# Gate and branch products of a hybrid layer with tokens in the partitions, and one attention head beside each 512 gate columns

## The chip, the cores and the metric

The kernel runs on one core of one Trainium2 chip, and the metric is the device time of one execution in microseconds (us). The engines of a core are named as in the profile: PE (TensorE, matrix products; PEld is its loading of weights), DVE (VectorE), ACT (ScalarE), POOL (GpSimd) and SP (SyncE, which here only issues DMA transfers). Each engine runs its instructions in the order in which they stand in its queue; semaphores hold an instruction until what it reads is there and what it overwrites is no longer needed. Products accumulate in PSUM, which has eight banks of 512 float32 per partition; the kernel uses four as a rotating pool `acc`, and twice two as `aux0` and `aux1`.

## The reference

One layer of a hybrid backbone, for 256 latent tokens `x` and 256 context tokens, model width 2048. Everything is float32. What matters here is the merge of the two branches:

```python
h_l = modulate(rms_norm(x, norm1_w), sh1, sc1)
...                                   # gated linear attention -> ya (256 x 1024)
...                                   # differential attention, 8 heads of 128 -> yb (256 x 1024)
def merge(h, ya, yb):
    g_a, g_b = jnp.split(jax.nn.sigmoid(h @ w_gate + b_gate), 2, axis=-1)
    return (g_a * (ya @ w_proj_gla) + g_b * (yb @ w_proj_diff)) @ w_out
mix_l = merge(h_l, gla_out(...), diff_out(o_diff))
x_new = x + g1 * mix_l
x_new = x_new + g2 * conv_ffn(modulate(rms_norm(x_new, norm2_w), sh2, sc2), ...)
```

The gate product is 256 x 2048 by 2048 x 4096, the two projections together 256 x 2048 by 2048 x 2048 (the upper half of the contraction belongs to `ya`, the lower to `yb`), and `w_out` is 2048 x 2048. The modulation vectors `g1`, `sh2`, `sc2`, `g2` come from a product of the conditioning vector with `w_ada`, which DVE computes as dot products beside all other work.

## The kernel before

**Products in two halves.** Each float32 weight tile is split into a high half (`whi`, a cast on ACT, L206) and a low half (`wlo`, a subtraction on DVE, L213, in `split`), 512 columns at a time; activations are split in the same way. A product is high by high, high by low and low by high. Weights come through `fetch` (L225) in transfers of 512 KB, four buffers deep; the halves have four buffers each.

**Two forms.** `col_tile` (L238) makes 128 output columns, with these columns in the partitions: the weight half is the stationary operand, and one product of 512 columns (L262, `whi` with both halves of the 256 tokens side by side) and one of 256 (L264, `wlo`) make a contraction step of 128. The two halves of the bank are added later. `row_tile` (L276) makes 512 output columns for 128 tokens, with the tokens in the partitions: the activation is stationary and the weights stream, in three products of 512 columns. The values of both attentions (`dv_chunk`, L961, with `value_rows`) and the last stage (`down`) use this second form; queries, keys, gates, projections, `w_out` and the up stage use the first.

**The stages around the change.** `dv_chunk(0)`, four query tiles (`dq_tile`), `dv_chunk(1)`; then for each of the eight heads the attention (`scores`, L1001; `attend`, L1025) at a high priority for the scheduler, a further query tile after each of the first four, and three gate tiles (`gate_tile`, L1049); then the eight gate tiles that are left. The scheduler orders the instructions of each engine by program order, priority and its own estimate of times, so the order on the engines is not that of the source. Each `gate_tile` puts its sum plus the bias into half of a tile `C`, by ACT and DVE. Four tiles `ks` of the attention share their places with `C12` to `C15`, and all `C` tiles take the places of the context activations (`c0` to `c15`), which `dv_chunk(1)` reads last. Then `ya` is made from the linear attention's output and its gate (`ge`, L1091 to L1097), and for each of 16 blocks of 128 columns `col_tile` makes both projections (`pga`, `pgb`); sigmoid, two multiplications (one on POOL) and a sum follow, and `merged` (L1101) splits the sum into `A[c]`, the input of `w_out` (`mix`).

**Conditioning.** `ada_next(n)` (L672) adds n to a due count; for each whole one it issues a load of 512 KB of `w_ada` (`araw`, two buffers) on SP, and a dot product on DVE (L356) for the oldest load. Of the 128 such steps the gates take 21, by the table `GATE_ADA`.

Of the kernel before, what the change touches and what calls it, by code (L numbers as in the profile page):

```python
# [9 lines left out]
F32 = mybir.dt.float32  # L10
# [8 lines left out]
P = 128  # L19
# [29 lines left out]
for _n, _w in [("b_ada", 96), ("norm1", 16), ("norm2", 16), ("ba", 8), ("gonorm", 1), ("qnorm", 1),  # L49
               ("knorm", 1), ("donorm", 1), ("b_gate", 32), ("lam", 256), ("conv_w", 3 * 2 * FT),  # L50
               ("conv_b", 2 * FT)]:
    _VEC[_n] = (_o, _w)
    _o += _w
# [10 lines left out]
def _tiles(w, starts):  # L64

    k = w.shape[0]
    return np.ascontiguousarray(
        np.stack([w[:, s:s + P].reshape(k // P, P, P).transpose(1, 0, 2) for s in starts]))


# [4 lines left out]
def _lay_out(i):  # L75
# [19 lines left out]
    a["w_in"] = _tiles(w_in, starts)  # L95
    a["w_gate"] = _tiles(np.asarray(i["w_gate"])[0], range(0, 2 * D, P))
    pg, pd = np.asarray(i["w_proj_gla"])[0], np.asarray(i["w_proj_diff"])[0]
    a["w_proj"] = _tiles(np.concatenate([pg, pd], axis=0), range(0, D, P))
    a["w_out"] = _tiles(np.asarray(i["w_out"])[0], range(0, D, P))
# [19 lines left out]
        "donorm": np.asarray(i["diff_onorm_w"])[0][:, None],  # L119
        "b_gate": _vec_tiles(np.asarray(i["b_gate"])[0]),  # L120
        "conv_w": np.asarray(i["conv_w"])[0].reshape(3, 2 * FT, P).transpose(2, 0, 1).reshape(P, -1),
# [25 lines left out]
def layer_kernel(tc, I, out):  # L147
# [3 lines left out]
    with es:  # L151
# [129 lines left out]
        def value_rows(banks, ws, n, first, last, emptied):  # L281
# [12 lines left out]
            for t in range(4):  # L294
                for k, w in ws:
                    products(t, k, w)
                emptied(t)

# [396 lines left out]
        with tc.tile_pool(name="gla", bufs=1) as pg:  # L695
# [253 lines left out]
        with tc.tile_pool(name="diff", bufs=1) as pd:  # L949
# [11 lines left out]
            def dv_chunk(j):  # L961
# [7 lines left out]
                for q in turn:  # L969
# [78 lines left out]

            def gate_tile(j):  # L1049
                ada_next(GATE_ADA[len(gates)])  # L1050
                b = acc_bank("gate")
                col_tile(I["w_gate"][j], A, b)
                if j == len(C):
                    C.append(hp.tile([P, 2, T], F32, tag=f"c{j}", name=f"C{j}"))
                gates[j] = C[j % KT][:, j // KT, :]
# [7 lines left out]
            dv_chunk(1)  # L1063
            order = [j for k in range(KT) for j in (k, KT + k)]
# [35 lines left out]

        def merged(c, earlier):  # L1101
            i = V.tensor_tensor(gates[c], gates[c], gates[16 + c], op=ALU.add)
            after(i, earlier)
            split_act(A[c][:, 1, :], A[c][:, 0, :], gates[c])

        for c in range(KT):
            ba, bb = acc_bank("pga"), acc_bank("pgb")
            col_tile(I["w_proj"][c, :, 0:8, :], yap, ba)
            col_tile(I["w_proj"][c, :, 8:16, :], ybp, bb)
            for j in (c, 16 + c):  # L1110
                sigs.append(S.activation(gates[j], gates[j], AF.Sigmoid))
                after(sigs[-1], sigm)
                after(sigs[-1], copied[0])
            for b, j in ((ba, c), (bb, 16 + c)):
                t = p3.tile([P, T], F32, tag="pt", bufs=2, name="pt")
                i = added(t, b)
                (G if j > c else V).tensor_tensor(gates[j], t, gates[j], op=ALU.mult)
                if j == c and c:
                    merged(c - 1, i)
            if c < KT - 2:  # L1120
                ada_next(13 / (KT - 2))
        merged(KT - 1, i)
        ada_done(0)

# [239 lines left out]
```

## Time and profile before

| what | value |
|---|---|
| median of 3 runs | 1691.38 us (1690.87 to 1692.67) |
| the profiled execution | 1692.95 us, span of its instructions 1690.6 us |
| `dv_chunk(1)` and start of head 0 | up to 537.7 us (last `dvb`) |
| gate products | 542.6 to 775.5 us |
| projections | 775.8 to 865.0 us |
| `w_out` (`mix`) | 865.3 to 956.1 us |

The rows of the profile name a line, an engine, an operation and output<-inputs by the program's names. A row of groups ends in busy time and mean duration, then the idle time before the group and its cause. Products are pipelined: the end of each is modelled, and neighbours overlap, so the pace of a stream is read from starts and counts, and not from durations.

### The profile page before, as it was taken

The page shows a single profiled execution, that of the slowest core. Times are in us where ns is not written, and L with a number is a line of the kernel's source. Part 1 is how long each engine was busy: PE and PEld are TensorE (multiplying, and loading weights), DVE is VectorE, ACT ScalarE, POOL GpSimd, SP SyncE. Part 2 cuts the span into 40 slices and gives each one's busy share as a digit, 9 for nine tenths or more (in the row PEclk, how much of TensorE's full clock was granted, in tenths as well). Part 3 has the DMA queues.
Part 4 walks back from the last instruction along what each step waited for, and adds up shares of the span by engine and source line. Part 5 has one row for each costly group of instructions (what it writes and reads, how often), then busy time and mean ns, then how long its engine had stood idle before and what let it go on. Part 6 is the DMA issues. An engine that isn't in the chain of part 4 may idle for free.

```text
span 1690.6 us, 28643 instructions
## 1 busy us (share of the span) xinstructions
PE 1671.0 (99%) x10140; PEld 1442.3 (85%) x10140; DVE 1271.2 (75%) x2426; ACT 977.7 (58%) x1980; POOL 329.0 (19%) x431
## 2 busy tenths in 40 slices
PE   7999999999999999999999999999999999999998
PEld 6779999998777888888888998888888888888887
DVE  5556765867787978788998797878888787755655
ACT  5324554756345867656766686666666666544443
POOL 0000213131210000001323200222222222684000
PEclk9999999999999999999999999999999999999999
DMA  9995532435566555688877566667777776676664
GB/s 384 403 408 195 171 133 85 150 100 166 173 212 223 171 192 187 211 273 277 272 261 260 181 198 218 227 227 237 238 236 237 225 240 219 202 222 207 217 195 142
DMA packets 110831, 370.82 MB, mean 219 GB/s; under 512 B 14433, under 2 KB 19553, under 8 KB 110689
## 3 DMA queue, kind: packets, MB, share of 16 engines
q1 hardware_dynamic: 102112, 362.51, 64.2%
q10 hardware_dynamic: 4032, 4.37, 0.8%
q0 software_dynamic: 4544, 2.14, 0.6%
q8 instruction: 79, 1.29, 0.3%
q14 instruction: 64, 0.52, 0.1%
HBM read 364.73 MB, written 2.10 MB: 217 GB/s over the span
## 4 chain that ended last, share of the span: by engine, by line
PE 92%; DVE 3%; DMA 3%; issue 1%; ACT 1%; POOL 0%; SPq 0%; DVEq 0%; POOLq 0%; ACTq 0%
PE down L1317 14%; PE upg L262 9%; PE upv L262 9%; PE gate L262 7%; PE sweep L368 5%; PE upv L264 5%; PE upg L264 5%; PE gate L264 4%; PE mix L262 4%; PE ab L368 2%; PE mix L264 2%; PE pgb L262 2%; PE pga L262 2%; DMA araw<-in_w_ada 2%; PE dk L333 2%; PE dk L332 2%
## 5 line engine op out<-in xcount | busy, mean ns | idle before, releaser
L206 ACT CAST whi<-wraw 128x512 fp32r<-128x512 f32 (+2 forms) x1004 | 607.1, 608 | 386.6 <-DVE wlo L213 111.3
L213 DVE TENSOR_TENSOR wlo<-wraw,whi 128x512 fp32r<-128x512 f32 (+2 forms) x932 | 635.5, 690 | 224.3 <-ACT whi L206 217.0
L262 PE MATMUL upg<-a,whi 128*128 128x512 f32 x656 | 229.0, 391 | 0.0
L262 PE MATMUL upv<-a,whi 128*128 128x512 f32 x656 | 229.0, 391 | 0.0
L1317 PE MATMUL down<-whi,g 128*128 128x512 f32 x704 | 216.9, 389 | 0.0
L264 PE MATMUL upv<-a,wlo 128*128 128x256 f32 x656 | 182.8, 280 | 0.0
L264 PE MATMUL upg<-a,wlo 128*128 128x256 f32 x656 | 182.6, 280 | 0.0
L262 PE MATMUL gate<-a,whi 128*128 128x512 f32 x512 | 179.9, 397 | 0.0
L213 POOL TENSOR_TENSOR wlo<-wraw,whi 128x512 fp32r<-128x512 f32 x72 | 100.3, 1393 | 388.0 <-ACT whi L206 375.2
L356 DVE CUSTOM_DVE_ANT_0 araw<-araw,cb 128x1024 f32<-128x1024 f32 x128 | 160.4, 1254 | 12.5 <-DMA araw<-in_w_ada 12.5
L1317 PEld LDWEIGHTS down<-whi,g 128*128 128x128 f32 x704 | 132.1, 188 | 27.5
L262 PEld LDWEIGHTS upv<-a,whi 128*128 128x128 f32 x656 | 122.4, 187 | 26.6
L262 PEld LDWEIGHTS upg<-a,whi 128*128 128x128 f32 x656 | 122.4, 187 | 26.5
L264 PE MATMUL gate<-a,wlo 128*128 128x256 f32 x512 | 141.0, 285 | 0.0
L1317 PE MATMUL down<-wlo,g 128*128 128x512 f32 x352 | 136.9, 389 | 0.0
L264 PEld LDWEIGHTS upv<-a,wlo 128*128 128x128 f32 x656 | 123.9, 189 | 0.5
L264 PEld LDWEIGHTS upg<-a,wlo 128*128 128x128 f32 x656 | 123.9, 189 | 0.5
L262 PEld LDWEIGHTS gate<-a,whi 128*128 128x128 f32 x512 | 94.4, 188 | 19.8 <-issue 0.4
L264 PEld LDWEIGHTS gate<-a,wlo 128*128 128x128 f32 x512 | 96.6, 189 | 6.6 <-issue 1.9
L262 PE MATMUL mix<-a,whi 128*128 128x512 f32 x256 | 89.1, 397 | 0.0
L1317 PEld LDWEIGHTS down<-wlo,g 128*128 128x128 f32 x352 | 66.1, 188 | 13.6
L1290 POOL DMA_DIRECT2D row<-turned x128 | 69.3, 549 | 30.0 <-DVE turned L1286 18.1
(351 smaller groups left out, 3396.6 us busy)
## 6 DMA issues: line engine op xcount, KB each, us to landing
wraw<-in_w_up SPq DMA_DIRECT2D x164, 512.0 KB, 4.4
araw<-in_w_ada SPq DMA_DIRECT2D x128, 512.0 KB, 4.9
wraw<-in_w_down SPq DMA_DIRECT2D x88, 512.0 KB, 4.3
ada<-in_w_ad SPq DMA_DIRECT2D x64, 512.0 KB, 10.0
wraw<-in_w_gate SPq DMA_DIRECT2D x64, 512.0 KB, 4.5
wraw<-in_w_in SPq DMA_DIRECT2D x58, 512.0 KB, 4.0
wraw<-in_w_proj SPq DMA_DIRECT2D x32, 512.0 KB, 4.8
wraw<-in_w_out SPq DMA_DIRECT2D x32, 512.0 KB, 4.6
```

Of the source, the lines that this page charges most:

```text
L206: copied[0] = S.copy(hi[:, :n], raw)
L213: i = e.tensor_tensor(lo[:, :n], raw, hi[:, :n].bitcast(F32), op=ALU.subtract)
L262: i = PE.matmul(b.rearrange("p (a b) -> p a b", a=2), whi[:, sl], acts[k], start=first, stop=last)
L264: i = PE.matmul(b[:, T:], wlo[:, sl], acts[k][:, 1, :], start=False, stop=last)
L332: PE.matmul(o, whi[:, sl], lo[k], start=False, stop=False)
L333: i = PE.matmul(o, wlo[:, sl], hi[k], start=False, stop=last and j == 1)
L356: i = V.tensor_tensor_reduce(raw, raw, cb[:, q * 1024:(q + 1) * 1024], 1.0, 0.0, op0=ALU.mult, op1=ALU.add, accum_out=ada2[:, j, q:q + 1])
L368: return kept(PE.matmul(*args, **kw))
L1290: nc.gpsimd.dma_start(to[32 * (q % 4):32 * (q % 4 + 1), :, 32 * p:32 * (p + 1)], turned[32 * p:32 * (p + 1), :, 32 * q:32 * (q + 1)])
L1317: i = PE.matmul(banks[h][t][n], g[:, a, ts], w[n][b], start=k == 0 and (a, b) == (1, 0), stop=k == FT - 1 and b == 1)
```

## The change

Gates and projections go from the first form to the second. `gate_rows` makes eight chunks of 512 gate columns (in the order of the blocks: gate a, gate b of the first 512 channels, then of the next) for two times 128 tokens; `token_rows` takes one transfer of two contraction steps, splits it and makes 2 x 2 x 3 products of 512 columns. The bias is now along the free dimension, so it is loaded, repeated over the partitions, into the `C` tile (16 loads of 256 KB on SP), and one DVE addition of 512 columns per bank takes the place of ACT's and DVE's two of 256. One head stands beside each chunk, and the priority of the heads falls from 500 to 150. In the projections, four blocks of 512 columns for each branch are multiplied with the sigmoids on DVE alone; the merged sum then has the tokens in the partitions, and `turned` brings it back with 32 transposes on PE (`mT`, 128 x 128) from which `A` is split. The conditioning steps are spread anew: 0.75 in place of 0.5 per transfer of the GLA values, 12 in place of 8 in `dv_chunk(0)`, 12 in place of 16 in `dv_chunk(1)`, 21 evenly in the gates, 9 in place of 13 in the projections.

```diff
-GATE_ADA = [0.25] * 4 + [0.5] * 16 + [1] * 12
+GATE_ADA = [21.01 / 64] * 64
...
+        def token_rows(src, banks, acts, k0, first, last, emptied):
+            raw = fetch(src.rearrange("p a b -> p (a b)"), 1024)
+            def products(t, k, w):
+                hi, lo = [{k: acts[k][:, u, :]} for u in (1, 0)]
+                row_tile(banks[t], k, *w, slice(0, 512), hi, lo, slice(t * P, (t + 1) * P), k == first, k == last)
+            if k0 + 1 != last:
+                for a in range(2):
+                    w = split(raw[:, a * 512:(a + 1) * 512], 512)
+                    for t in range(2):
+                        products(t, k0 + a, w)
+                return
...
-                    ada_next(0.5)
+                    ada_next(0.75)
...
-                            if j or q > 3:
-                                ada_next(1)
+                            if j or q > 1:
+                                ada_next(0.75 if j else 1)
...
-            def gate_tile(j):
-                ada_next(GATE_ADA[len(gates)])
-                b = acc_bank("gate")
-                col_tile(I["w_gate"][j], A, b)
...
-                S.activation(gates[j], b[:, :T], AF.Identity, bias=vcol("b_gate", j))
-                V.tensor_tensor(gates[j], b[:, T:], gates[j], op=ALU.add)
+            def gate_rows():
+                for n in range(8):
+                    g = n // 2 + 4 * (n % 2)
+                    banks = [acc_bank("gate") for _ in range(2)]
+                    def emptied(t):
+                        V.tensor_tensor(gates[g, t], banks[t], gates[g, t], op=ALU.add)
+                    for q in range(8):
...
+                        if q == 5:
+                            for t in range(2):
+                                C.append(hp.tile([P, 2, T], F32, tag=f"c{len(C)}", name=f"C{len(C)}"))
+                                gates[g, t] = C[-1].rearrange("p a b -> p (a b)")
+                                nc.sync.dma_start(gates[g, t], I["b_gate"][:, g * 512:(g + 1) * 512])
+                        token_rows(I["w_gate"][g, q], banks, A, 2 * q, 0, KT - 1, emptied)
+                        yield
...
-                with tc.high_priority(500):
+                with tc.high_priority(150):
...
-                for _ in range(3):
-                    gate_tile(order.pop(0))
-            while order:
-                gate_tile(order.pop(0))
+                for _ in range(8):
+                    next(gating)
...
+        def turned(c):
+            for u in range(2):
+                b = aux_bank("mT", u)
+                for j in range(2):
+                    for t in range(2):
+                        PE.transpose(b[:, j * T + t * P:j * T + (t + 1) * P],
+                                     gates[c, t][:, (2 * u + j) * P:(2 * u + j + 1) * P], ident)
+                for j in range(2):
+                    a = A[4 * c + 2 * u + j]
+                    split_act(a[:, 1, :], a[:, 0, :], b[:, j * T:(j + 1) * T])
+        for c in range(4):
+            for part, acts in enumerate((yap, ybp)):
...
+                def emptied(t):
+                    V.tensor_tensor(gates[g, t], banks[t], gates[g, t], op=ALU.mult)
+                    if part:
+                        V.tensor_tensor(gates[c, t], gates[c, t], gates[g, t], op=ALU.add)
+                for q in range(4):
+                    if 8 * c + 4 * part + q < 28:
+                        ada_next(9.01 / 28)
+                    token_rows(I["w_proj"][c, 4 * part + q], banks, acts, 2 * q, 0, HEADS - 1, emptied)
+                if c and not part:
+                    turned(c - 1)
+        turned(3)
```

Three places of the engines' order show what the scheduler makes of it. First PE, in the gate stage beside a late head, before the change (`oss` is the sum for a head's norm, `s` its scores):

```order
L262 MATMUL gate<-a_1380,whi 128x512
L264 MATMUL gate<-a_1380,wlo 128x256
L614 MATMUL oss<-osqs,ones 128x256
L615 MATMUL oss<-osqs,ones 128x256
L1009 MATMUL s<-ks,qs 128x512 x6
L264 MATMUL gate<-a_1450,wlo 128x256
```

And PE beside one of the last three heads after the change:

```order
L1036 MATMUL s<-ks,qs 128x512 x2
L283 MATMUL gate<-whi,a_402 128x512
L1036 MATMUL s<-ks,qs 128x512
L284 MATMUL gate<-whi,a_402 128x512
L1036 MATMUL s<-ks,qs 128x512
L283 MATMUL gate<-whi,a_402 128x512
L1036 MATMUL s<-ks,qs 128x512
L284 MATMUL gate<-whi,a_402 128x512
L1036 MATMUL s<-ks,qs 128x512
L285 MATMUL gate<-wlo,a_402 128x512 x2
```

The six score products of a block, which stood together, now stand one by one between gate products; the gate products are all 512 wide, with the activation as the stationary operand.

Second PE, at the start of `w_out` after the change, where the last quarter of the merged sum is turned (`C_8175` and `C_8177` are its two halves of tokens); ahead of these rows stand 24 products of the first `mix` tile, on the quarters that are turned already:

```order
L268 MATMUL mix<-a_1133,whi 128x512
L270 MATMUL mix<-a_1133,wlo 128x256
L268 MATMUL mix<-a_219,whi 128x512
L1145 MATMUL mT<-ident,C_8175 128x128 x2
L1145 MATMUL mT<-ident,C_8177 128x128
L1145 MATMUL mT<-ident,C_8175 128x128
L1145 MATMUL mT<-ident,C_8177 128x128 x2
L1145 MATMUL mT<-ident,C_8175 128x128
L1145 MATMUL mT<-ident,C_8177 128x128
L270 MATMUL mix<-a_219,wlo 128x256
L268 MATMUL mix<-a_330,whi 128x512
```

The transposes moved behind the first products of `w_out`, with a second `mix` tile (from `a_219` on) taken in after them.

Third SP, late in `dv_chunk(1)` and at the first gate weights, after the change (`C_...` are the bias loads into the places of context tiles):

```order
L1095 DMA C_6981<-in_b_gate 128x512
L377 DMA araw<-in_w_ada 128x1024
L1095 DMA C_7335<-in_b_gate 128x512
L233 DMA wraw<-in_w_gate 128x1024
L1095 DMA C_7337<-in_b_gate 128x512
L377 DMA araw<-in_w_ada 128x1024
L1095 DMA C_7613<-in_b_gate 128x512
L233 DMA wraw<-in_w_gate 128x1024
L377 DMA araw<-in_w_ada 128x1024
L1095 DMA C_7615<-in_b_gate 128x512
L1095 DMA C_7894<-in_b_gate 128x512
L1095 DMA C_7896<-in_b_gate 128x512
```

Twelve of the sixteen bias loads stand here, ahead of the use of their tiles by up to six chunks; before the change SP had only weights and conditioning loads at this place.

More of the change, by code (lines that the diff above doesn't have):

```diff
@@ L49 @@
 for _n, _w in [("b_ada", 96), ("norm1", 16), ("norm2", 16), ("ba", 8), ("gonorm", 1), ("qnorm", 1),
-               ("knorm", 1), ("donorm", 1), ("b_gate", 32), ("lam", 256), ("conv_w", 3 * 2 * FT),
+               ("knorm", 1), ("donorm", 1), ("lam", 256), ("conv_w", 3 * 2 * FT),
                ("conv_b", 2 * FT)]:
@@ L68, in _tiles, with _row_tiles @@
         np.stack([w[:, s:s + P].reshape(k // P, P, P).transpose(1, 0, 2) for s in starts]))
+def _row_tiles(w):
+    k, n = w.shape
+    return np.ascontiguousarray(w.reshape(k // (2 * P), 2, P, n // 512, 512).transpose(3, 0, 2, 1, 4))
 def _vec_tiles(v):
@@ L95, in _lay_out @@
     a["w_in"] = _tiles(w_in, starts)
-    a["w_gate"] = _tiles(np.asarray(i["w_gate"])[0], range(0, 2 * D, P))
+    a["w_gate"] = _row_tiles(np.asarray(i["w_gate"])[0])
+    a["b_gate"] = np.tile(np.asarray(i["b_gate"])[0][None], (P, 1))
     pg, pd = np.asarray(i["w_proj_gla"])[0], np.asarray(i["w_proj_diff"])[0]
-    a["w_proj"] = _tiles(np.concatenate([pg, pd], axis=0), range(0, D, P))
+    a["w_proj"] = _row_tiles(np.concatenate([pg, pd], axis=0))
     a["w_out"] = _tiles(np.asarray(i["w_out"])[0], range(0, D, P))
@@ L119, in _lay_out @@
         "donorm": np.asarray(i["diff_onorm_w"])[0][:, None],
-        "b_gate": _vec_tiles(np.asarray(i["b_gate"])[0]),
         "conv_w": np.asarray(i["conv_w"])[0].reshape(3, 2 * FT, P).transpose(2, 0, 1).reshape(P, -1),
@@ L296, in value_rows @@
                     products(t, k, w)
+                emptied(t)
+        def token_rows(src, banks, acts, k0, first, last, emptied):
[9 more added lines that the diff above has]
+                return
+            ws = [split(raw[:, a * 512:(a + 1) * 512], 512) for a in range(2)]
+            for t in range(2):
+                for a in range(2):
+                    products(t, k0 + a, ws[a])
                 emptied(t)
@@ L1047, in layer_kernel @@
             gates, ya, yb = {}, {}, {}
-            def gate_tile(j):
-                ada_next(GATE_ADA[len(gates)])
-                b = acc_bank("gate")
-                col_tile(I["w_gate"][j], A, b)
-                if j == len(C):
-                    C.append(hp.tile([P, 2, T], F32, tag=f"c{j}", name=f"C{j}"))
-                gates[j] = C[j % KT][:, j // KT, :]
-                S.activation(gates[j], b[:, :T], AF.Identity, bias=vcol("b_gate", j))
-                V.tensor_tensor(gates[j], b[:, T:], gates[j], op=ALU.add)
+            def gate_rows():
+                steps = 0
+                for n in range(8):
[4 more added lines that the diff above has]
+                    for q in range(8):
+                        if q in (1, 2):
+                            flush((later, latest)[q - 1])
+                        ada_next(GATE_ADA[steps])
+                        steps += 1
+                        if q == 5:
[5 more added lines that the diff above has]
+                        yield
             nts = norm_tiles()
@@ L1063, in layer_kernel @@
             dv_chunk(1)
-            order = [j for k in range(KT) for j in (k, KT + k)]
+            gating = gate_rows()
             with tc.high_priority(500):
@@ L1099, in layer_kernel @@
         yap, ybp = [[y[h].rearrange("p (a b) -> p a b", a=2) for h in range(HEADS)] for y in (ya, yb)]
[L1101 to L1121, printed above, removed]
@@ L1122, in layer_kernel @@
-        merged(KT - 1, i)
+        def turned(c):
+            for u in range(2):
+                b = aux_bank("mT", u)
+                for j in range(2):
+                    for t in range(2):
+                        PE.transpose(b[:, j * T + t * P:j * T + (t + 1) * P],
[3 more added lines that the diff above has]
+                    split_act(a[:, 1, :], a[:, 0, :], b[:, j * T:(j + 1) * T])
@@ new lines, in layer_kernel @@
+        for c in range(4):
+            for part, acts in enumerate((yap, ybp)):
+                banks = [acc_bank("pg") for _ in range(2)]
+                g = c + 4 * part
+                for t in range(2):
+                    sigs.append(S.activation(gates[g, t], gates[g, t], AF.Sigmoid))
+                    after(sigs[-1], sigm)
+                    after(sigs[-1], copied[0])
+                def emptied(t):
[8 more added lines that the diff above has]
+                    turned(c - 1)
```

## The prediction

> **What bounds the kernel now.** I read the page first: busy shares, slices, chain of waits.
>
> ```profile
> span 1690.6 us, 28643 instructions
> PE 1671.0 (99%) x10140; PEld 1442.3 (85%) x10140; DVE 1271.2 (75%) x2426; ACT 977.7 (58%) x1980; POOL 329.0 (19%) x431
> ...
> PEclk9999999999999999999999999999999999999999
> ...
> PE 92%; DVE 3%; DMA 3%; issue 1%; ACT 1%; POOL 0%; SPq 0%; DVEq 0%; POOLq 0%; ACTq 0%
> ```
>
> TensorE is busy for all but 20 us, at the full clock, and 92% of the chain is its own work. So two things count: what the change adds to or takes from TensorE's stream of products, and what is left of the short idle times. Work removed from other engines gains nothing by itself. Next, the busy times by stretch: the first chunk of values (`dv_chunk(0)`), the second chunk of values (`dv_chunk(1)`) with the first head, the heads beside gate tiles, gate tiles alone, the projections, the output projection.
>
> ```profile
> 400.00:458.00 58.00, 57.07 (x314) 45.33 (x312) 37.18 (x68) 21.15 (x43) 13.87 (x25) 1.00 0.55 182
> ...
> 484.00:541.00 57.00, 54.65 (x253) 42.53 (x252) 45.51 (x95) 25.74 (x55) 1.62 (x2) 1.00 0.74 237
> 542.60:702.00 159.40, 158.12 (x914) 133.77 (x913) 134.20 (x302) 117.26 (x256) 10.18 (x10) 1.00 0.57 185
> 705.00:775.00 70.00, 70.00 (x400) 60.85 (x399) 56.45 (x104) 42.17 (x79) 0.00 (x0) 1.00 0.83 277
> 775.80:865.20 89.40, 89.40 (x513) 78.19 (x512) 84.87 (x165) 63.41 (x144) 23.58 (x15) 1.00 0.78 260
> ```
>
> Columns: length, then busy time (instructions) of PE, PEld, DVE, ACT, POOL; clock, DMA share, GB/s. The reader is to see that PE idles 0.9, 2.4 and 1.3 us in the first three stretches, nothing in the others, and that DVE is at 95% in the projections and still nobody waits for it.
>
> **Part 1, pace of the gate products.** Before, one contraction step of 128 gate columns is a pair: a product 512 wide and one 256 wide. After, one step of 512 columns is six products, all 512 wide. Four pairs and six products stream the same 3072 columns; only the price of a product beside its columns can differ. Gate tiles alone:
>
> ```profile
> L262 PE MATMUL gate<-a,whi 128*128 128x512 f32 x199 | 69.4, 398 | 0.0
> L264 PE MATMUL gate<-a,wlo 128*128 128x256 f32 x199 | 53.9, 281 | 0.0
> L615 PE MATMUL oss<-osqs,ones 128*128 128x256 f32 x1 | 0.3, 281 | 0.0
> L614 PE MATMUL oss<-osqs,ones 128*128 128x256 f32 x1 | 0.3, 279 | 0.0
> ```
>
> In these 70 us stand 199 pairs and two sums of 0.12 us: (70 - 0.24) / 199 = 350.6 ns a pair. (The mean durations, 398 and 281 ns, overlap and are not the pace.) The form that the change uses exists elsewhere: the values (`dvb`, stretch 484 to 496) and the last stage (`down`); the up stage has the pair form:
>
> ```profile
> 484.00:496.00 12.00, 11.57 (x51) 1.00 0.81 245
> 1040.00:1400.00 360.00, 360.00 (x2078) 1.00 0.71 232
> 1460.00:1680.00 220.00, 220.00 (x973) 1.00 0.65 203
> ```
>
> `dvb`: 11.57 / 51 = 226.9 ns; `down`: 220 / 973 = 226.1; a pair in the up stage: 360 / 1039 = 346.5. So a pair costs 346.5 to 350.6 where one and a half wide products cost 340. Before: 32 tiles x 16 pairs x 350.6 = 179.5 us. After: 8 chunks x 16 steps x 6 x 0.227 = 174.3. **Minus 5.2 us**; bounds: minus 5.9 at 226.1 ns, and nothing if the surplus belongs to this stage and not to the form.
>
> The Trainium skill (TensorE: Matmul & The Clock Gate, Back-to-back issue gap) gives N/2.4 + 2.5 ns for a product of N columns in a stream: 215.8 and 109.2 here, so 325.0 a pair and 323.7 for one and a half wide ones. By it the gates would gain 0.7 us instead of 5.2; the rows are dearer than both and put the pair 10 ns above, so I keep the rows.
>
> **Part 2, projections and transposes.**
>
> ```profile
> L262 PE MATMUL pga<-ya,whi x128: 391/394/398, 775.8 to 862.5; 128*128 128x512 f32 x128
> ...
> L262 PE MATMUL mix<-a,whi x256: 387/397/403, 865.3 to 956.1; 128*128 128x512 f32 x128
> 596.85 0.60 PE L1034 MATMUL pT<-ident,pe 128*128 128x128 f32 x4
> 597.20 0.36 PE L264 MATMUL dq<-a,wlo 128*128 128x256 f32 x1
> 597.40 0.40 PE L262 MATMUL dq<-a,whi 128*128 128x512 f32 x1
> ```
>
> Before: 865.3 - 775.8 = 89.5 us for 256 pairs. After: 4 x 2 x 8 x 6 = 384 products x 0.227 = 87.2, and 32 transposes of the merged sum. From the start of four transposes to the second product behind them are 0.55 us, of which 0.12 belong to the one narrow product; so 0.43 for four, 0.108 each, 3.5 us for 32. Sum 90.7: **plus 1.2 us** (plus 0.9 to plus 3.5, if the wide form gains nothing). The last eight transposes stand behind the first 24 products of `mix` in PE's order, 4.2 us, which cover the multiply, add and casts that they wait for; I cost that wait at nothing, at most 1 us.
>
> The Trainium skill (same page, Part 4: PE-mode transpose) gives about 275 ns for a 128x128 transpose in a kernel. That would make 8.8 us of the 32; the row's spacing of 0.108 is a stream's, and the longer time is in the trace only as the length of one alone (rival e).
>
> **Part 3, scores torn apart.** The score products use half the array's rows, and two of them (maps 0 and 1) run at once when they stand side by side:
>
> ```profile
> 608.97 0.28 PE L614 MATMUL oss<-osqs,ones 128*128 128x256 f32 x1
> 609.09 0.28 PE L615 MATMUL oss<-osqs,ones 128*128 128x256 f32 x1
> 609.30 0.96 PE L1009 MATMUL s<-ks,qs 64*128 64x512 f32 x6
> 610.19 0.38 PE L264 MATMUL gate<-a,wlo 128*128 128x256 f32 x1
> ```
>
> From 609.09 to 610.19, less one sum of 0.12, six products take 0.98 us: three slots of 0.227 and 0.30 for entering and leaving the half-array form. With the lower priority the scheduler puts gate products between them. In PE's order I count 15 unbroken runs with 48 slots before (one of twelve products, the rest of six), and 28 runs with 55 slots after: heads 5 to 7 are torn to single products. Seven slots x 0.227 = 1.6; 13 more runs at 0.18 (a lone product, my estimate: 0.30 less the changes inside a run) = 2.4. **Plus 4.0 us**; 1.6 if entering alone costs nothing, 5.5 at 0.30.
>
> **Part 4, stalls.** Where PE idles in 484 to 541:
>
> ```profile
> DVE araw L356 <- DMA araw<-in_w_ada: 10.0, 9, 2.1
> ...
> PEld dvb L279 <- DVE wlo L213: 2.4, 4, 1.3
> PEld dvb L277 <- ACT whi L206: 2.3, 2, 1.9
> ```
>
> DVE stands 10 us in its queue at conditioning dots (`araw`) whose load has not landed; the low halves and the score maxima queue behind, and PE's weight loads wait 4.7 us. The change lowers the dots due in this chunk from 16 to 12 and moves four to the first chunk, where DVE was busy 64% (37.18 of 58); the GLA values take four from the projections. I take back half: **minus 2.5 us** (0 to minus 4.7). Late next is the copy of the transposed probabilities ahead of the first head's output, where the order is unchanged and the idle time stays:
>
> ```profile
> 548.13 0.60 PE L1034 MATMUL pT<-ident,pe 128*128 128x128 f32 x4
> 550.01 1.78 PE L1040 MATMUL o<-pT,dv 128*128 128x256 f32 x7 [1.28 <-ACT pT L1035]
> ...
> wraw<-in_w_gate SPq DMA_DIRECT2D x64, 512.0 KB, 4.5
> ```
>
> On SP the scheduler hoists 12 of the 16 bias loads (256 KB) among the last value and conditioning loads; each waits for the context tile whose place it takes, the last (`C11`) for the end of the values. Behind it wait the gate weights of step 4 on, which PE reaches 14 us later (a query tile 5.6, 24 gate products 5.4, scores, outputs and sums 3); a landing of 4.5 us (last row above) and a cast fit, so nothing. Their 3 MB over some 35 us add 90 GB/s to 237, at a DMA share of 0.74.
>
> **Part 5, the hand-over to the projections.** Before, `ya` was made beside eight gate tiles without attention (70 us). After, the last head runs inside the last two chunks. DVE, in 705 to 775:
>
> ```profile
> L213 DVE TENSOR_TENSOR wlo<-wraw,whi 128x512 fp32r<-128x512 f32 x49 | 32.8, 688 | 6.6 <-ACT whi L206 5.6
> L356 DVE CUSTOM_DVE_ANT_0 araw<-araw,cb 128x1024 f32<-128x1024 f32 x13 | 15.9, 1219 | 1.0 <-DMA araw<-in_w_ada 1.0
> ...
> L232 DVE TENSOR_TENSOR ya<-ge,ya 128x256 fp32r<-128x256 f32 x8 | 3.1, 418 | 0.0
> L1094 DVE TENSOR_TENSOR ge<-oy,ge 128x512 f32<-128x512 f32 x4 | 2.7, 687 | 0.0
> ```
>
> From the last gate chunk to step 6 of the first projection (22 steps, 22 x 6 x 0.227 = 30.0 us of PE) DVE's order holds about 20 low halves (13.8), 4 dots with their read-out (5.2), 4 gate sums of 512 (2.8, priced as `ge`), 3 `ge` (2.1), 6 `ya` (2.5) and 5 small ones of the last head (2.2): 28.6. It fits barely. **Plus 0.8 us** (0 to 3).
>
> DVE and ACT lose 32 bias passes, the POOL products and 32 copies; PE waits for none of these in the stretches above: nothing.
>
> **Sum.** -5.2 + 1.2 + 4.0 - 2.5 + 0.8 = -1.7 us on an execution of 1692.95 (span 1690.6 and 2.35 around it): 1691.2. The median of the runs, 1691.38, lies 1.6 lower, so 1689.7 is forecast: **no change that a measurement can tell** (0.2% is 3.4 us, about what one resolves here).
>
> **Rivals.** (a) Faster: the dots were the whole cause of the stall (-4.7), and the torn scores cost only their slots (+1.6): -6.3, 1685.1. For it: 9 of DVE's waits name that load. Against: the added single runs. Chance 0.28.
> (b) Slower: the pair's surplus is this stage's and not its form's, so the six wide products take 233.7 ns (two thirds of 350.6). Gates gain 0, projections lose 3.7 (384 x 0.2337 + 3.5 - 89.5): with the scores PE +7.7, in all +6.0, 1697.4. It decides from about 231.5 ns on: 4.5 ns over 227 on 1152 products are 5.2 us, which turn -1.7 into +3.5. For it: the up stage's pair is 4 ns cheaper. Against: `dvb` keeps 226.9 with DMA at 0.81. The Trainium skill's formula above, by which wide products gain almost nothing, would end here. Chance 0.12.
> (c) Slower, at the hand-over: two of the four `gr` tiles are still to be made when the first projection starts; if their chain (DVE: 0.69 + 2 x 0.42 = 1.5, ACT's sigmoid and casts taken as the same) is late as a whole, PE waits 2 x 3.0 us in place of 0.8: +3.5, 1694.9. It decides once DVE or ACT is over four steps behind, the depth of the weight buffers. Chance 0.08.
> (d) The heads are not spread and the time stays: PE's order speaks against it; 0.02, inside "same".
> (e) Transposes don't stream but cost a single one's length (0.60 less three spacings of 0.108: 0.28), 8.8 us for 32 in place of 3.5: +3.6, 1695.0. Against: the spacing row. The Trainium skill's 275 ns would be this case. Chance 0.02.
>
> **Numbers.** Forecast 0.50 with (d), its own range 1686.5 to 1693; (a) 0.28; (b) 0.12; (c) 0.08; (e) 0.02. Range 1684.5 to 1696.5. Of the forecast's half, 0.02 ends below 1688.0 (0.2% under the median): faster 0.30, same 0.48, slower 0.22.
>
> **What would show it.** `gate` and `pg` near 227 ns a product (part 1); proj start to `mix` start about 90.7 us; `mT` at 0.108; `s` in single rows of 0.4 us in the last heads; PEld's waits for `dvb` under 2.5 us in the second value chunk and `araw` waits well under 10; no PE wait at the first `pg`. Wrong if gate products take over 231 ns, if PE idles at the first `pg`, or if SP's bias loads hold weights back.

## The result, and the profile after

| kernel | median (lowest to highest) | ratio to the kernel before (95% interval) |
|---|---|---|
| before | 1691.94 us (1690.87 to 1693.68, 11 runs) | 1 |
| after | 1695.78 us (1695.17 to 1698.05, 11 runs) | 1.0025 (1.0018 to 1.0033) |

The change makes the kernel 3.8 us slower, 0.25%, and the interval leaves out zero. The forecast was 1689.7, 1.7 us faster, and called that no change; its own range ended at 1693. The time lies inside the whole range (1684.5 to 1696.5), but on the side that had the smallest chance, and for reasons that no rival named. The profiled execution of after took 1695.55 us, its span is 1693.7. The page and the busy times by stretch (columns as before: length, then PE, PEld, DVE, ACT, POOL with instructions; clock, DMA share, GB/s):

```profile
span 1693.7 us, 27919 instructions
PE 1673.9 (99%) x9788; PEld 1426.9 (84%) x9788; DVE 1257.9 (74%) x2370; ACT 957.4 (57%) x1900; POOL 304.2 (18%) x415
...
PE 96%; DVE 2%; DMA 1%; ACT 1%; issue 0%; SPq 0%; DVEq 0%
```

```profile
400.00:458.00 58.00, 56.83 (x314) 45.38 (x312) 41.38 (x75) 20.20 (x41) 16.02 (x25) 1.00 0.65 209
...
484.00:541.00 57.00, 57.00 (x267) 44.78 (x266) 45.35 (x93) 28.14 (x60) 1.62 (x2) 1.00 0.80 267
542.00:702.00 160.00, 158.70 (x756) 126.80 (x754) 133.63 (x286) 104.55 (x220) 7.97 (x10) 1.00 0.65 211
735.00:775.00 40.00, 40.00 (x181) 33.16 (x180) 31.14 (x57) 25.81 (x47) 0.00 (x0) 1.00 0.79 264
775.70:867.40 91.70, 91.70 (x409) 74.60 (x408) 70.17 (x120) 53.00 (x97) 0.00 (x0) 1.00 0.71 228
```

The clock is full in both kernels. TensorE's busy time rose by 2.9 us, nearly the whole loss, on fewer instructions; its idle time in the span stayed (19.6 and 19.8 us). So the loss is not a new wait, at least not in the sum. (A product that is held up between its neighbours counts as busy, so "57.00 of 57" can still hide lost time.) The stretch 484 to 541 shows the stall of the second value chunk gone: 2.35 us of idle time before, none now. The first chunk (400 to 458) is the other way round: DVE 41.4 us busy in place of 37.2, and TensorE a little less.

Where the time went is read from the first starts of each stage, which the views of one tile (`gate`, `pg`, `mix`; columns: shortest, median and longest duration in ns, first and last start) and TensorE's timeline give:

```profile
L283 PE MATMUL gate<-whi,a x256: 387/389/580, 542.0 to 774.8; 128*128 128x512 f32 x128
...
L283 PE MATMUL pg<-whi,ya x64: 388/394/404, 775.7 to 855.6; 128*128 128x512 f32 x64
...
L268 PE MATMUL mix<-a,whi x256: 389/395/403, 867.4 to 958.5; 128*128 128x512 f32 x128
...
460.05 0.53 PE L268 MATMUL dq<-a,whi 128*128 128x512 f32 x1 [2.12 <-DVE osq L333]
```

and before the change

```profile
458.62 0.50 PE L262 MATMUL dq<-a,whi 128*128 128x512 f32 x1 [1.51 <-DVE osq L306]
```

| stretch (first start to first start) | before | after | difference |
|---|---|---|---|
| start to first query tile after the first value chunk (`dq`) | 458.6 | 460.05 | +1.4 |
| `dq` to first gate (query tiles, second value chunk, head 0) | 84.0 | 81.95 | -2.1 |
| first gate to first projection (gates and heads) | 233.2 | 233.7 | +0.5 |
| projections, to first `mix` | 89.5 | 91.7 | +2.2 |
| `mix` to the end of the span | 825.3 | 826.3 | +1.0 |

The stretches don't hold quite the same work: after the change, four pairs of query products more (153 `dq` products in place of 145, 1.4 us at 0.35 a pair) and six score products fewer (24 in place of 30, 1.0 us) stand ahead of the first gate, and eight transposes (0.9 us, worked out below) stand behind the first `mix`.

The gate stage hides two large terms in one small difference: cheaper products, and the heads' scores. The next timeline is TensorE beside head 7 (start and duration in us; a row is a product or a run of them):

```profile
701.38 0.40 PE L285 MATMUL gate<-wlo,a 128*128 128x512 f32 x1
701.71 0.49 PE L1036 MATMUL s<-ks,qs 64*128 64x512 f32 x2
702.13 0.49 PE L283 MATMUL gate<-whi,a 128*128 128x512 f32 x1
702.56 0.50 PE L1036 MATMUL s<-ks,qs 64*128 64x512 f32 x1
702.99 0.50 PE L284 MATMUL gate<-whi,a 128*128 128x512 f32 x1
703.42 0.50 PE L1036 MATMUL s<-ks,qs 64*128 64x512 f32 x1
...
705.55 0.50 PE L285 MATMUL gate<-wlo,a 128*128 128x512 f32 x1
```

From 701.38 to 705.55, 4.17 us, pass five gate products (5 x 0.227 = 1.14) and the six score products of one block: 3.03 us, where a block that stands together took 0.98 (the prediction's rows at 609). Of the 2.05 us more, two further slots (a slot is the 0.227 us of one product of 512 columns, which two score products side by side share) are 0.45; the other 1.6 belong to four further runs (unbroken rows of score products), **0.40 us a run**. Neighbours start 0.43 us apart, 0.20 over the pace, at the change into the half-array form and again at the change out of it. TensorE's weight loads at the same place:

```profile
700.92 0.19 PEld L284 LDWEIGHTS gate<-whi,a 128*128 128x128 f32 x1
701.15 0.19 PEld L285 LDWEIGHTS gate<-wlo,a 128*128 128x128 f32 x1
701.70 0.19 PEld L1036 LDWEIGHTS s<-ks,qs 64*128 64x128 f32 x2 [0.36 <-ACT pT L1062]
702.13 0.19 PEld L283 LDWEIGHTS gate<-whi,a 128*128 128x128 f32 x1 [0.24 <-issue]
702.55 0.18 PEld L1036 LDWEIGHTS s<-ks,qs 64*128 64x128 f32 x1 [0.24 <-issue]
702.99 0.19 PEld L284 LDWEIGHTS gate<-whi,a 128*128 128x128 f32 x1 [0.25 <-issue]
```

In the stream a load runs one product ahead (the load at 701.15 is for the product at 701.38). At each change of form it idles 0.24 us and is recorded at the start of its own product (702.13 and 702.13): the load is no longer hidden, and its 0.19 us is about the 0.20 lost. The Trainium skill (TensorEngine Tiling (Array Packing), Tiling Modes) says that changing the tiling mode drains TensorE; the trace agrees in that no load runs ahead at a change, and 0.2 us are lost there.

Below, "the time around `s`" is a sum over a whole trace: from the start of each of the 96 score products to the next start, plus, for the products beside them, what their distance exceeds the pace of their width. It is 17.5 us before and 24.2 us after, **6.7 us more**, where the prediction had 4.0.

### The profile page after: what moved, and what is told of

Its sections match the earlier page's. It is cut to its first block, busy times and chain, and to the rows that moved or that the text cites. A ratio compares the mean times of both kernels' runs of the same rounds, so it can differ in the third digit from the quotient of the medians.

```text
span 1693.7 us, 27919 instructions
## 1 busy us (share of the span) xinstructions
PE 1673.9 (99%) x9788; PEld 1426.9 (84%) x9788; DVE 1257.9 (74%) x2370; ACT 957.4 (57%) x1900; POOL 304.2 (18%) x415
## 4 chain that ended last, share of the span: by engine, by line
PE 96%; DVE 2%; DMA 1%; ACT 1%; issue 0%; SPq 0%; DVEq 0%
PE down L1366 14%; PE upg L268 9%; PE upv L268 9%; PE sweep L395 5%; PE upv L270 5%; PE upg L270 5%; PE gate L285 4%; PE mix L268 4%; PE gate L283 3%; PE gate L284 3%; PE ab L395 2%; PE mix L270 2%; PE pg L283 2%; PE pg L284 2%; PE pg L285 2%; PE dk L360 2%
## 5 line engine op out<-in xcount | busy, mean ns | idle before, releaser
L283 PE MATMUL gate<-whi,a 128*128 128x512 f32 x256 | 101.1, 395 | 0.0
L284 PE MATMUL gate<-whi,a 128*128 128x512 f32 x256 | 100.2, 392 | 0.0
L285 PE MATMUL gate<-wlo,a 128*128 128x512 f32 x256 | 88.4, 400 | 0.0
L270 PE MATMUL mix<-a,wlo 128*128 128x256 f32 x256 | 69.1, 280 | 0.0
```

The costliest lines, as they stand in the source:

```text
L270: i = PE.matmul(b[:, T:], wlo[:, sl], acts[k][:, 1, :], start=False, stop=last)
L283: PE.matmul(o, hi[k][:, ts], whi[:, sl], start=first, stop=False)
L284: PE.matmul(o, lo[k][:, ts], whi[:, sl], start=False, stop=False)
L285: return PE.matmul(o, hi[k][:, ts], wlo[:, sl], start=False, stop=last)
```

## The experiments

The theories to be told apart: (1) the torn scores cost 6.7 us, by the changes of form; (2) the projections' products run at 232 ns, not 227, for a reason that lies in their stationary operand, and not in traffic; (3) the conditioning dots moved into the first value chunk cost what stands in the table's first row, and their going is what freed the second chunk. Ratios are to the kernel before, on the same chip, whose median in each of the two sets of timed runs was 1692.12 us. Three of the four tests of the projections are single executions, and their traces alone are read.

### Scores together again, by the heads' priority

```diff
             for h in range(HEADS):
-                with tc.high_priority(150):
+                with tc.high_priority(500):
                     scores(h, 1)
```

> The kernel after the change, with the heads' priority back at 500. In TensorE's order the score products then stand in 17 unbroken runs of 48 slots, in place of 28 runs of 55. Theory 1 (the torn scores are what made the kernel slower: in the trace of after all time around `s` products sums to 24.2 us, before to 17.5 us): the sum falls to 17.5 to 18.5 us, the gate stage from 233.7 to about 228, and the time from 1695.8 to 1689.5 to 1690.5 us. Rival (the wide gate products slow down beside any attention work, or the heads cost as much wherever they stand): the time stays within 1 us of 1695.8, and the gate stage within 1 us of 233.7.

Measured: 1689.53 us, 0.9985 (0.9976 to 0.9993). The time around `s` is 19.7 us and the gate stage 227.4 us (541.14 to 768.52). Theory 1 gave 1689.5 to 1690.5, and the time is that; the rival (within 1 us of 1695.8) falls. But the sum around `s` fell by 4.5 of the 6.7 only (17.5 to 18.5 was expected), so not all of the 6.2 us gained is this, and that the time fits is partly luck. The trace is that of an execution of 1687.88 us, 1.6 below the median, and its gate stage gained 6.3 us. Waits don't explain the rest: the one for the transposed probabilities in front of the first head's output is gone, but one for a high half came in its place. PE's waits in 541 to 776, of after and of this kernel:

```profile
PE o L1067 <- ACT pT L1062: 1.3, 1, 1.3
```

```profile
PE gate L283 <- ACT whi L212: 1.5, 1, 1.5
```

### Only the scores at the high priority

```diff
-                with tc.high_priority(150):
+                with tc.high_priority(500):
                     scores(h, 1)
+                with tc.high_priority(150):
                     attend(h, 0)
                     if h + 1 < HEADS:
                         halves(h + 1)
-                        scores(h + 1, 0)
+                with tc.high_priority(500):
+                    if h + 1 < HEADS:
+                        scores(h + 1, 0)
+                with tc.high_priority(150):
                     attend(h, 1)
```

> The kernel after the change, with only the score products at priority 500, and the rest of each head left at 150: 15 runs of 48 slots, as before the change, while transposes, sums and outputs of the heads stay spread among the gate products. Theory 1: the time around `s` falls from 24.2 to about 17.5 us, and the kernel to 1689 to 1690 us; as fast as with the whole head at 500, or up to 1 us faster. Rival (the other parts of a head lose as much by being spread as the scores): 1692.5 to 1695, clearly above the kernel with the whole head at 500.

Measured: 1687.08 us, 0.9968 (0.9956 to 0.9981), 2 us below the expected 1689 to 1690; the rival's 1692.5 to 1695 falls. The time around `s` is 17.3 us, as before the change, and PE has no wait at all in 541 to 776. A block beside head 2:

```profile
599.64 0.40 PE L284 MATMUL gate<-whi,a 128*128 128x512 f32 x1
599.97 0.96 PE L1036 MATMUL s<-ks,qs 64*128 64x512 f32 x6
600.86 0.73 PE L285 MATMUL gate<-wlo,a 128*128 128x512 f32 x2
```

From 599.64 to 600.86 less one gate product of 0.227: 0.99 us for six scores, against 3.03 in the torn block. Scores -6.9, the wait ahead of the first output (1.3 by the row above, 1.5 with what the product loses beside it) and 0.4 at the first `dq` (459.6) sum to 8.8. The medians differ by 8.7 (1695.78 - 1687.08), the spans of the two profiled executions by 7.7 (1693.7 - 1686.0), so the sum is right to about 1 us. The rest of a head may be spread among the gate products; only the scores may not.

### Conditioning dots back out of the first value chunk

```diff
-GATE_ADA = [21.01 / 64] * 64
+GATE_ADA = [25.01 / 64] * 64
...
-                            if j or q > 1:
+                            if j or q > 3:
                                 ada_next(0.75 if j else 1)
```

> The kernel after the change with 8 conditioning dots in the first chunk of values, as before the change, in place of 12; the four go to the gates (25 in place of 21). The second chunk keeps its 12. The order also tears the scores a little less (23 runs of 52 slots in place of 28 of 55), worth 5 x 0.4 + 3 x 0.23 = 2.7 us less at the price that theory 1 gives. Theory 3 (the four dots moved into the first chunk cost it 1.4 us by DVE's queue): the first `dq` product starts at about 458.6 us of the span in place of 460.05, the second chunk keeps its gain, and the time is 1695.8 - 1.4 - 2.7, about 1691.5 to 1692.5 us. Rival (the first chunk lost by chance of one load's landing, not by the dots): first `dq` at 460, time 1693 to 1694.5.

Measured: 1690.74 us, 0.9992 (0.9983 to 1.0001); first `dq` at 458.38, the time around `s` 21.2. So 1.7 us came back before `dq`, and 3.0 from the scores: 4.7 of the 5.0 measured. The first `dq` came where theory 3 put it (458.6) and not where the rival did (460); the time is 0.8 below theory 3's range. PE's waits from 440 to 462, of after and then of this kernel:

```profile
PE dq L268 <- DVE osq L333: 2.1, 1, 2.1
PE sc L857 <- DVE e L889: 1.1, 1, 1.1
```

```profile
PE dq L268 <- DVE osq L333: 1.5, 1, 1.5
```

and what DVE did in after ahead of that `sc`:

```profile
446.28 1.22 DVE L383 CUSTOM_DVE_ANT_0 araw<-araw,cb 128x1024 f32<-128x1024 f32 x1 [2.64 <-DMA araw<-in_w_ada]
...
448.76 0.68 DVE L889 TENSOR_TENSOR e<-e,qk 128x512 f32<-128x512 f32 x1
```

A dot whose load had not landed held DVE's queue for 2.64 us, and the linear attention's `e` behind it came late for TensorE. DVE was under three quarters busy in this stretch (41.4 of 58), which did not matter: the cost lies in what stands behind the dot in the queue.

How much it costs varies from kernel to kernel with the same dots, so the rival was not all wrong. From the first `dvb` to the first `dq` the profiled executions of all kernels with 8 dots here took 58.3 to 58.4 us (before, this one and three of the kernels below); those of the seven with 12 dots took 58.8 to 60.0, 59.8 in after and 59.5 in the mean. Four dots more cost 0.5 to 1.7 us.

### The old forms with fewer dots in the second value chunk

```diff
-GATE_ADA = [0.25] * 4 + [0.5] * 16 + [1] * 12
+GATE_ADA = [0.5] * 12 + [0.75] * 12 + [1.26] + [1.25] * 7
...
                             if j or q > 3:
-                                ada_next(1)
+                                ada_next(0.75 if j else 1)
```

> The kernel before the change, with one edit: 12 conditioning dots in place of 16 in the second chunk of values, four more in the gates (25 in place of 21). Theory 3 (fewer dots take away the 2.4 us in which TensorE waited there): TensorE idles under 0.7 us in the second chunk of values, and the time falls by 1.5 to 2.5 us, to about 1689.4 to 1690.4 beside a 1691.9 of before. Rival (the stall goes in the changed kernel for another reason, such as the SP order with the bias loads): the idle time stays near 2.4 us and the time within 0.6 us of before.

Measured: 1687.84 us, 0.9977 (0.9968 to 0.9986), 4.3 us faster than the kernel before, twice what was expected.

```profile
484.00:541.00 57.00, 57.00 (x277) 46.01 (x277) 47.95 (x104) 31.40 (x67) 2.27 (x3) 1.00 0.64 213
```

TensorE's 2.35 us of idle time are gone, with 277 instructions done here where there were 253. DVE's waits for `araw` fell from 10.0 to 1.2 us. The idle time alone was too low an estimate of the gain. From the first `dq` to the first gate the kernel takes 82.0 us in place of 84.0, with four pairs of query products and four transposes more in it, 1.4 and 0.4 us of work: 3.9 us came from this stretch, where 2.35 stood as idle time (a product that is held up counts as busy). Behind it the 1.3 us wait in front of the first output is gone, with 0.8 us of waits for low halves in its place, and from `mix` to the end of the span 1.2 us are lost, for a reason not followed up. So this part of the change, alone, is a gain, and it needs neither the new form nor the bias loads.

### The old forms with the heads at the lower priority

```diff
             for h in range(HEADS):
-                with tc.high_priority(500):
+                with tc.high_priority(150):
                     scores(h, 1)
```

> The kernel before the change with one edit: the heads' priority from 500 to 150. The gates keep their first form. The score products then stand in 26 runs of 51 slots in place of 15 of 48. From after: 6.7 us for 13 runs and 7 slots, less 7 x 0.227, are 0.39 us a run. Theory 1 (the price lies in each change between score products and other products, whatever their form): 11 x 0.39 + 3 x 0.227 = 5.0 us, the time around `s` from 17.5 to about 22.5, the kernel at about 1697. Rival (only wide products with a stationary activation pay for a score product among them): 17.5 to 19, the kernel at 1691.5 to 1693.5.

Measured: 1693.2 us, 1.0006 (0.9998 to 1.0015). The time around `s` rose to 22.2, by 4.7, as theory 1 gave; the rival's 17.5 to 19 falls, so the price is the change between the forms, also where the other product is the old pair. But the kernel as a whole lost 1 us, which its interval does not tell from nothing, and not 5: the time lies where the rival put it (1691.5 to 1693.5), and it is the sum around `s` that decides. My expectation counted the scores alone. The lower priority pays part of the 5 us back in the second value chunk:

```profile
484.00:541.00 57.00, 57.00 (x257) 43.86 (x256) 47.55 (x97) 27.55 (x59) 1.62 (x2) 1.00 0.74 249
```

```profile
L356 DVE CUSTOM_DVE_ANT_0 araw<-araw,cb 128x1024 f32<-128x1024 f32 x15 | 18.9, 1258 | 7.0 <-DMA araw<-in_w_ada 6.8
```

DVE still waits 6.8 us for the conditioning loads, at 15 dots, and yet TensorE does not idle; nor does it in front of the first output, since PE has no wait from 541 to 776 here. So in these traces fewer dots free the second chunk, and so does a lower priority with nearly all the dots left: it took both the late loads and the heads' early place to starve TensorE. The changed kernel has both remedies, and part (3) of the theories is only half of the cause.

### The projections' products: four tests of the 232 ns

The mean distance from one `pg` product's start to the next in after is 232.0 ns (377 distances; those over 260 ns, with a change of form or a missing record between, are left out), against 228.1 for `gate` and 226.7 for `down`, taken in the same way. The median durations in the rows above show it too: 394 ns for `pg`, 389 for `gate`. First, another stationary operand:

```diff
-            for part, acts in enumerate((yap, ybp)):
+            for part, acts in enumerate(([A[12 + k % 4] for k in range(8)],) * 2):
```

> The kernel after the change, with another stationary operand in the projections: they multiply four tiles of the normalised input (A12 to A15) and not the branch outputs ya and yb, so what is computed differs from the reference there; count, form and order of the products stay. Theory 2 (the place from which TensorE loads the activations sets the pace: the projections' wide products take 232.0 ns from the places of ya and yb, the gates' 228.1 from A): the projections' products fall to 227 to 228 ns, first projection to first `mix` from 91.74 to about 90.0 us, the time to about 1694. Rival (traffic of the other engines beside the projections, or what the products of this stage write to, sets it): 231.5 to 232.5 ns as before, and the time within 0.6 us of 1695.8.

Measured: 226.8 ns, the projections 89.8 us (774.9 to 864.7), 1694.26 us. The executions spread from 1691.8 to 1698.7 us, so the pace decides and not the time. The rival falls.

```profile
L283 PE MATMUL pg<-whi,a x128: 389/389/398, 774.9 to 863.7; 128*128 128x512 f32 x128
...
L268 PE MATMUL mix<-a,whi x256: 389/395/403, 864.7 to 955.9; 128*128 128x512 f32 x128
```

Then the traffic, by taking the conditioning out of the stage:

```diff
-GATE_ADA = [21.01 / 64] * 64
+GATE_ADA = [30.01 / 64] * 64
...
-                        ada_next(9.01 / 28)
+                        ada_next(0)
```

> The kernel after the change with no conditioning step due in the projections: their nine loads and dots go to the gates (30 in place of 21). Theory of the traffic (transfers and DVE work beside the projections slow their products to 232.0 ns): without 4.6 MB of loads and 11 us of DVE's dots they fall to 229.5 ns or less, and the gates' rise from 228.1 to about 229. Theory 2 (the place of the stationary operand): both stay, 231.5 to 232.5 and 228 to 228.5 ns. The time itself tells little here, since the scores are torn a little differently (28 runs, 56 slots).

Measured: 232.0 ns for `pg`, 228.4 for `gate` (1695.79 us, one run). The traffic of the nine steps has no part in it. Then the values of the operand, left in the places of `ya` and `yb`:

```diff
-                split_act(yb[h][:, T:], yb[h][:, :T], o)
+                S.copy(yb[h][:, T:], A[12 + h % 4][:, 1, :])
+                V.tensor_copy(yb[h][:, :T], A[12 + h % 4][:, 0, :])
...
-                split_act(ya[h][:, T:], ya[h][:, :T], e[:, j * T:(j + 1) * T])
+                S.copy(ya[h][:, T:], A[12 + h % 4][:, 1, :])
+                V.tensor_copy(ya[h][:, :T], A[12 + h % 4][:, 0, :])
```

> The kernel after the change, where the tiles ya and yb are filled with copies of both halves of A12 to A15, by one ACT and one DVE pass each as before; the projections read ya and yb in their places, so what is computed differs from the reference in the projections' input. This tells apart what taking the operand from A12 to A15 left open, place or values. Theory of the place: the projections' products stay at 231.5 to 232.5 ns. Theory of the values: 226.5 to 227.5 ns. The whole time tells little, since the scores are torn a little differently (27 runs, 54 slots).

```profile
L283 PE MATMUL pg<-whi,ya x64: 388/394/404, 773.6 to 853.5; 128*128 128x512 f32 x64
```

Measured: 232.1 ns (1693.25 us, one run). The values are not it. Last, four tiles in place of sixteen:

```diff
-            for part, acts in enumerate((yap, ybp)):
+            for part, acts in enumerate(([yap[k % 4] for k in range(8)],) * 2):
```

> The kernel after the change, where all projections multiply ya0 to ya3 (four tiles in place of sixteen, as with A12 to A15, but in the places of ya), so what is computed differs from the reference there. This tells apart what is left of the place: how many tiles the operand is taken from, or where they lie. Theory of the address: the projections' products stay near the 230.3 to 233.2 ns that the places of ya0 to ya3 have in after, 232 in the mean. Theory of the count of tiles: 226.5 to 227.5 ns, as from A12 to A15. The whole time tells little.

Measured: 232.7 ns (1694.86 us, one run). So it is where the operand lies: the same values take 5 ns a product less from `A` than from the tiles of `ya` and `yb`. What about the place does it stays open. No run here moved these tiles, and they are also laid out differently (516 columns long, where a tile of `A` has 512). TensorE's weight loads have a mean of 188 ns in `pg` in both cases, so the 5 ns don't show in the record of the load.

### The parts that gain, together

The changed forms with only the scores at the high priority and with 8 dots in the first value chunk (the diffs of the second and third experiment together):

> The changed kernel's forms with whole score blocks (only the scores at priority 500: 15 runs, 48 slots) and with 8 dots in the first chunk of values, 12 in the second, 25 in the gates. If the two causes add: 1687.1 (scores alone) less about 1.1 (first `dq` at 458.5 in place of 459.6) gives 1685 to 1686.5, 1.5 to 2.5 us below the old forms with the same dots (1687.8): the gates' -5.3, the projections' +2.3 and the small stalls. If the form change is worth nothing once the scores stand together: 1687.5 to 1688.5, level with the old forms with the same dots.

Measured: 1686.9 us, 0.9971 (0.9959 to 0.9982): 5 us faster than the kernel before and 9 us faster than the one after the change. The time lies between the two expected ranges (1685 to 1686.5, and 1687.5 to 1688.5), so neither is borne out. It stands level with the second experiment (0.9968), whose interval it shares, so the dots' 1.1 us could not be shown in the time; the first `dvb` product of its profiled execution stood at 401.1, 1.5 us later than in the second experiment's (399.6), for a reason ahead of the edits that set the two apart, and from there to the first `dq` it took 58.3 us against 60.0. Against the old forms with the same number of dots in both value chunks (1687.84) the new forms are worth 0.9 us, with intervals that overlap: by TensorE's own sum -4.4 for the gates and +3.1 for projections and transposes (both worked out below), that is -1.3. So what the new forms are worth by themselves was not told from nothing in the time.

## Why the prediction was wrong

**Part 1, the gates' pace (-5.2): held, a little small.** `gate` took 228.1 ns a product over the stage, so 768 products are 175.2 us against 179.5: -4.3 to -4.4. The surplus was the form's, as forecast, and not the stage's. (The Trainium skill, TensorE: Matmul & The Clock Gate, Back-to-back issue gap, gives the prediction's formula for an isolated product, and about 131 ns for 512 columns in a stream; neither is what is seen here, 226.7 to 232.7 ns.)

**Part 2 (+1.2): mis-sized.** The step that failed is "384 products x 0.227 = 87.2". They took 232.0, 1.9 us more, so the part came out at +3.1. The other half of the sum held: the transposes stand in the stream at about the forecast 0.108, and the last eight cost no wait.

```profile
804.45 1.03 PE L1145 MATMUL mT<-ident,C 128*128 128x128 f32 x8
805.24 0.71 PE L285 MATMUL pg<-wlo,ya 128*128 128x512 f32 x2
805.80 0.39 PE L283 MATMUL pg<-whi,ya 128*128 128x512 f32 x1
```

From 804.45 to 805.80 less two wide products (0.454) are 0.90 us for eight, 0.112 each. The Trainium skill's 275 ns for a transpose, weighed in the prediction, is not the price in this stream. Rival (b) had a slower wide product in both stages, from 231.5 ns on; only the projections passed that, and their reason was one no rival held.

**Part 3 (+4.0): mis-sized, and the largest error.** The step is "13 more runs at 0.18 (a lone product, my estimate: 0.30 less the changes inside a run)". The count was right, the price 0.40. Two things were wrong in the 0.18. The 0.30 of a whole block is not all of its price: it was taken up to 610.19, where the product behind the block starts, but that product's load is not hidden either, and the next start comes 0.22 us later, where 256 columns take 0.12:

```profile
610.19 0.38 PE L264 MATMUL gate<-a,wlo 128*128 128x256 f32 x1
610.41 0.40 PE L262 MATMUL gate<-a,whi 128*128 128x512 f32 x1
```

So a whole block, too, costs 0.40 beside its slots, 0.20 for each change of form. And there was nothing to take off for a lone product: it has the same two changes. The sign that the prediction gave, "`s` in single rows of 0.4 us", did come (0.43 from its start to the next), but the gate product behind it pays the same again. Seven slots at 0.227 and 13 runs at 0.39 are the 6.7 measured, above the upper bound of 5.5. A bound that would have held it stood in the profile of before, in the weight loads of 484 to 541 (the last numbers are busy us, mean ns and idle us):

```profile
L278 PEld LDWEIGHTS dvb<-whi,c 128*128 128x128 f32 x32 | 6.0, 188 | 1.3
```

Two loads of 188 ns that nothing hides are 0.38 us a run: 13 x 0.38 + 7 x 0.227 = 6.5.

**Part 4 (-2.5): the gain right, the cost left out.** The stall of the second value chunk is gone in full (-2.35 in the window). But "moves four to the first chunk, where DVE was busy 64%" was costed at nothing, and cost 1.4 us (0.5 to 1.7 over the kernels run). The share of busy time said nothing of a dot that waits for its load ahead of the linear attention's work. The stall that I called late next, ahead of the first output, stayed as forecast (1.3 us of wait), and the bias loads on SP held nothing back: with them TensorE is busy through 484 to 541.

**Part 5 (+0.8): nothing.** PE has no wait in 775 to 868; rival (c) did not come.

The sum with the measured prices: -4.4 + 3.1 + 6.7 - 2.35 + 1.4 = +4.5, against +3.1 between the two spans and +3.8 between the medians. What is left, 1.4 us by the spans and 0.7 by the medians, was not followed up. No term had the wrong sign. Three costs were too small (by 2.7, 1.9 and 1.4) and the gates' gain was too large by 0.8, all in one direction; only part 5 erred by 0.8 in the other. Rival (a), the likeliest after the forecast, assumed that torn scores cost only their slots; the opposite was the case. Of the costs, 8.1 us hang on two settings, the one priority for a whole head and the four dots in the first chunk. The scores' 6.7 come back in the time without the first; the dots' 1.4 come back in the length of the first chunk (58.3 us in place of 59.8), but in the time the kernel with both settings undone is level with the one that has the first alone undone.

## What to carry to other kernels

Products that use part of the array's rows should stand together: count the changes of form in TensorE's order, each at an unhidden weight load, before lowering a priority that keeps them apart from the rest. A dot or copy that waits for a load belongs where nothing urgent stands behind it on its engine; the engine's share of busy time does not tell this, its queue does. And an expected pace should be taken from products that read the same operand from the same place, since the place alone was worth 2% here.

## What the runs showed of the hardware that was not expected

- A change between the half-array and the full form costs 0.18 to 0.20 us on TensorE, in each direction, with either form of the other products: 4.7 us for 11 runs and 3 slots more with the old pairs, 6.7 us for 13 runs and 7 slots with wide products.
- The stationary operand's place sets the pace of a stream of wide products at full clock: 226.8 ns from four tiles of `A`, 232.0 to 232.7 from the tiles of `ya` and `yb`, whatever the values, the number of tiles and the conditioning traffic. Whether the address or the layout of the tiles does it was not told apart.
